# Sums of input-matrix products formed on TensorE by accumulated matmuls with the identity and its negative

## The chip, the core and the metric

The kernel runs on one NeuronCore of a Trainium2 chip. Five engines work from queues of their own and meet only at semaphores: TensorE (PE in the profile, with its weight loads as PEld), VectorE (DVE), ScalarE (ACT), GpSimd (POOL) and SyncE (SP), which here only issues DMAs. Each engine takes its instructions strictly in the order in which the program lists them. An instruction whose input isn't ready holds up all that stand behind it on the same engine. The metric is the device time of one execution in microseconds (us).

## What is computed

One encoder layer on a sequence of 1024 rows of 1024 numbers, in float32. The part that matters here is the state-space mixer (S5): the first 512 channels are cut into 32 groups of 16, each with 64 complex states in two directions.

```python
def s5_direction(uf, lam_re, lam_im, log_dt, b_re, b_im, c_re, c_im, reverse):
    ...
    lam_bar = jnp.exp(lam * dt)
    b = lax.complex(b_re.astype(f32), b_im.astype(f32))
    b_bar = ((lam_bar - 1.0) / lam)[..., None] * b
    c = lax.complex(c_re.astype(f32), c_im.astype(f32))
    bu = jnp.einsum('gph,blgh->blgp', b_bar, uf)
    a = jnp.broadcast_to(lam_bar, (1, uf.shape[1]) + lam_bar.shape)
    _, states = lax.associative_scan(_ssm_combine, (a, bu), reverse=reverse, axis=1)
    return jnp.einsum('ghp,blgp->blgh', c, states).real
...
def reference(x, ...):
    xn = rmsnorm(h, g_mix[i])
    proj = xn @ w_in[i]
    u = proj[..., :D_SSM]
    v = proj[..., D_SSM:]
    y_ssm = s5_mixer(u, ...)
    y_fft = fourier_mixer(v, w_fourier[i])
    h = h + jnp.concatenate([y_ssm, y_fft], axis=-1) @ w_out[i]
    h = h + conv_ffn(rmsnorm(h, g_ffn[i]), ...)
return rmsnorm(h, g_final)
```

The product of a complex factor with a complex input matrix has a real part that is a difference of two products and an imaginary part that is a sum of two products. These 2 x 16 differences and sums are what the change is about.

## The kernel before

The program is written as a list of steps, the string `SEQ`, whose tokens name a function and its arguments: `P:5` is `prep(5)`, `I:5` is `inputs(5)`, `S:5` is `states(5)`, `O:5` is `outputs(5)`, `U` and `VI` are products with the input projection, `WB` products with the output projection, `FA`, `FB`, `FC` the Fourier part. The order in which the steps are written gives each instruction its priority. A scheduler of the language then lays the instructions of each engine in a row by a timeline of its own, so the final order on each engine is fixed when the program is built and isn't read from the source. A second table, `OPT`, says of some 400 small operations whether they run on VectorE (`V`) or GpSimd (`G`).

The time falls into three stages. Up to about 81 us the input is normalised and transposed, the projection starts, and tables of the state-space poles are worked out. From 81 to about 335 us the state-space gather runs: 16 batches of two groups each, among products of the projections (tiles `pin` and `pwo` in PSUM) and the Fourier part. From there to the end follow the gate of the mixer (`pg`), the upward product of the feed-forward part (`u`), and the downward one (`dqa`, `dqb`).

In the gather a batch b goes through these steps. Buffer numbers are left out by the profile, so all batches show under one name.

- `prep(b)`, lines 658 to 683, is where the change lies. For the real part (i = 0) and the imaginary part (i = 1) a vector multiplication writes the products of the factor table `gst` and the raw matrix `rawb` into a tile `b` of 128x512 (line 666). It holds two halves of 256 columns. A second vector operation takes the difference or the sum of the halves into the tile `bt` (line 667); `bt` has one buffer. TensorE transposes the four 128x128 blocks of `bt` into the PSUM tile `pbm` (line 672), ScalarE copies it to `bm`. TensorE also multiplies each block of `bt` with `cbr` or `cbi`, the output matrices of the group, into `pk` (line 677, recorded as the helper's line 130), and ScalarE copies the result to `kf` and `kb`.
- `inputs(b)`: TensorE multiplies `bm` with the inputs `u` into `ps` (line 733).
- `states(b)`: VectorE multiplies `ps` with a phase table into `r` (line 745), adds halves into `scd`, runs four scans into `so` (lines 756 and 757), multiplies into `x` (line 763) and adds into `yy` (line 764). Some of these run on GpSimd.
- `outputs(b)`: TensorE forms `py` from `tm`, `u`, `yy` and the table `cm` (which `out_matrix` makes with `c` and `cm`, lines 721 to 725).

The tiles `b`, `r` and `x` take their buffers from one pool with the tag `t2`; a new tile waits until a buffer's last reader is done. Before, the tag has two buffers. All of `pbm`, `pk`, `ps` and `py` take turns in four PSUM banks. TensorE's order holds the `pin` and `pwo` matmuls, which depend on nothing in the gather, between the gather's own matmuls.

Of the kernel before, what the change touches and what calls it, by code (L numbers as in the profile page):

```python
# [11 lines left out]
F32 = mybir.dt.float32  # L12
# [3 lines left out]
AF = mybir.ActivationFunctionType  # L16
ALU = mybir.AluOpType
# [3 lines left out]
P = 128  # L21
# [9 lines left out]
LA = 4  # L31
NBM = 3
NTM = 2
NWP = 5
NSPLIT = 9
NTAB = 1026
# [45 lines left out]
def bc(ap, axis, n):  # L82
    ap = ap.unsqueeze(axis)
    shape = list(ap.shape)
    shape[axis] = n
    return ap.broadcast_to(shape)
# [3 lines left out]
def encoder_block(  # L90
# [8 lines left out]
    V, A, PE, GP = nc.vector, nc.scalar, nc.tensor, nc.gpsimd  # L99
# [3 lines left out]
    const = ctx.enter_context(tc.tile_pool(name="const", bufs=1))  # L103
# [5 lines left out]
    def opt(key, default):  # L109
        v = OPT.get(key, default)  # L110
        return {"V": V, "G": GP}.get(v, v) if isinstance(v, str) else v
# [7 lines left out]
    def bank2(name):  # L119
        return ps.tile([P, 512], F32, name=name, tag="bank_b")  # L120

    def after(ins, prev):
        tc.add_manual_dep(
            ins.ins, prev.ins.name,
            mybir.DependencyInfo(mybir.DependencyClass.NoSync, mybir.DependencyReason.DATA),
            reason="issue order",
        )

    def mm(o, lhsT, rhs, start, stop, key=None, skip=False):
        i = PE.matmul(o, lhsT, rhs, start=start, stop=stop, skip_group_check=skip)  # L130
        last_mm[0] = i
        if key is not None:
            if key in chain:
                after(i, chain[key])
            chain[key] = i
        return i
# [3 lines left out]

    ident = const.tile([P, P], F32, name="ident")
    make_identity(nc, ident)

    def gbc_dma(src, t):
        return nc.sync.dma_start(t, src.partition_broadcast(P))
# [7 lines left out]
    def split(dst_hi, dst_lo, src, eng=V):  # L153
        A.activation(dst_hi, src, AF.Copy)  # L154
        return eng.tensor_sub(dst_lo, src, dst_hi.bitcast(F32))  # L155
# [8 lines left out]
    def load_split(src, a, name, w=None, eng=V, g=None, geng=None):  # L164
# [10 lines left out]
        if w is None:  # L175
            w = outer.tile([P, 2, 512], F32R, name=name, tag="wp", bufs=NWP)
        split(w[:, 0], w[:, 1], st, eng)
# [71 lines left out]
    def q(name, shape=(P, G), dt=F32, tag="q", bufs=13):  # L249
        return sp.tile(list(shape), dt, name=name, tag=tag, bufs=bufs)  # L250

    def keep(name, shape=(P, G), dt=F32):
        return sp.tile(list(shape), dt, name=name)

    NG = 2
    NB = G // NG
# [83 lines left out]
    def pair(a):  # L340
        return a.rearrange("p (b g) -> p b g", g=NG)
# [4 lines left out]
    gst = keep("gst", (P, 8, NB, 3, NG))  # L346
# [35 lines left out]
    def cmul(eng, outr, outi, ar, ai, br_, bi_, ta, tb):  # L382

        eng.tensor_mul(ta, ar, br_)
        eng.tensor_mul(tb, ai, bi_)
        eng.tensor_sub(outr, ta, tb)
        eng.tensor_mul(ta, ar, bi_)
        eng.tensor_mul(tb, ai, br_)
        eng.tensor_add(outi, ta, tb)

    def csq(c, s_, name):

        a, b, c2, s2 = (q(f"{name}_{k}") for k in "abcs")
        V.tensor_sub(a, c, s_)
        V.tensor_add(b, c, s_)
        V.scalar_tensor_tensor(s2, c, 2.0, s_, ALU.mult, ALU.mult)
        V.tensor_mul(c2, a, b)
        return c2, s2
# [96 lines left out]
    def phase_tables(lv):  # L495
        wt_ = w1t if lv == 4 else w2t
        te = opt(f"ph{lv}", GP)
        if lv == 4:
            ec, es, ecn = (prv[k] for k in ("ec", "es", "ecn"))
            esd = q("esd")  # L500
            V.tensor_copy(esd[0:64], es[0:64])
            V.tensor_copy(esd[64:128], ecn[64:128])
            prv["cur"] = (ec, esd)
        cur = prv["cur"]
        wr, wi = wt_[:, :, 0], wt_[:, :, 1]
        if lv == 2:
            GP.memset(wr[:, :, :, 0], 1.0)
            GP.memset(wi[:, :, :, 0], 0.0)
        for j in range(lv):
            n = 1 << j  # L510
            tw = q(f"tw{lv}_{j}", (P, 2, NB, NG, 8), tag="t3" if te is GP else "t2", bufs=1 if te is GP else 2)
            cmul(te, wr[:, :, :, n:2 * n], wi[:, :, :, n:2 * n], wr[:, :, :, :n], wi[:, :, :, :n],
                 bc(pair(cur[0]), 3, n), bc(pair(cur[1]), 3, n), tw[:, 0, :, :, :n], tw[:, 1, :, :, :n])
            cur = csq(cur[0], cur[1], f"wq{lv}_{j}")
        prv["cur"] = cur
        if lv == 2:
            GP.tensor_copy(w2t[:, :, 2], w2t[:, :, 0])

    def in_factors():
        fr, fi = prv["fr"], prv["fi"]  # L520
        gt = q("gt", (P, 4, 8, G), tag="tm", bufs=NTM)
        gr_, gi_ = gt[:, 0], gt[:, 1]
# [6 lines left out]
    def out_factors():  # L529
        ec, ecn = prv["ec"], prv["ecn"]  # L530
        pt_ = q("pt", (P, 4, 8, G), tag="tm", bufs=NTM)
        cmul(V, pt_[:, 0], pt_[:, 1], pwr, pwi, bc(ec, 1, 8), bc(ecn, 1, 8), pt_[:, 2], pt_[:, 3])
# [6 lines left out]
    scd = keep("scd", (P, 2, NG, W))  # L539
    scr = keep("scr", (P, NG, W))  # L540
    cbr = keep("cbr", (P, 8, 2, 16))
    cbi = keep("cbi", (P, 8, 2, 16))

    def zeros():
        nc.sync.dma_start(dmk[96:128], dmask)
        for t in (scd, scr, cbr, cbi):
            GP.memset(t, 0.0)

    cw = const.tile([P, 188], F32, name="cw")
    rawb = keep("rawb", (P, NB, 2, NG, 16))  # L550
    rawc = keep("rawc", (P, NB, 2, NG, 16))
# [83 lines left out]
        cts[ct].u = u  # L635

    def t2(name):
        return q(name, (P, 2 * NG * P), tag="t2", bufs=2)

    def prep_ct(ct):  # L640

        for dst, i in ((cbr, 0), (cbi, 1)):
            for d in range(2):
                hs = slice(64 * d, 64 * d + 64)
                A.activation(
                    dst[hs, :, d].rearrange("p (b g) h -> p b g h", g=NG),
                    rawc[hs, 4 * ct:4 * ct + 4, i], AF.Copy)
        cts[ct].kf = q(f"kf{ct}", (P, 8, 16), tag="kf", bufs=1)
        cts[ct].kb = q(f"kb{ct}", (P, 8, 16), tag="kb", bufs=1)

    def slots(a, b, swap=0):

        return bc(a[:, :, b, swap:swap + 2].rearrange("p s i g -> p (i g) s"), 3, 16)

    def heads(a, b):
        return bc(a[:, b].rearrange("p i g h -> p (i g) h"), 2, 8)

    def prep(b):

        c, ct, sb = bs[b], b // 4, b % 4  # L660
        if sb == 0:
            prep_ct(ct)
        bt = q(f"bt{b}", (P, 2, NG, 8, 16), tag="bt", bufs=1)
        for i, op in ((0, ALU.subtract), (1, ALU.add)):
            m = t2(f"b{b}_{i}").rearrange("p (n s h) -> p n s h", n=2 * NG, s=8)
            opt(f"pb{b}{i}", V).tensor_mul(m, slots(gst, b, i), heads(rawb, b))
            opt(f"pa{b}{i}", V).tensor_tensor(bt[:, i], m[:, 0:NG], m[:, NG:2 * NG], op)
        c.bm = q(f"bm{b}", (P, 2, NG, P), tag="bm", bufs=NBM)
        pt = bank2(f"pbm{b}")
        btv = bt.rearrange("p i g s h -> p (i g) (s h)")  # L670
        for n in range(2 * NG):
            PE.transpose(pt[:, n * P:(n + 1) * P], btv[:, n], ident)
        A.activation(c.bm.rearrange("p i g n -> p (i g n)"), pt, AF.Copy)
        pk = bank2(f"pk{b}")
        for g in range(NG):
            for i, cc in ((0, cbr), (1, cbi)):
                mm(pk[:, g * 32:(g + 1) * 32], btv[:, i * NG + g],
                   cc[:, NG * sb + g].rearrange("p d h -> p (d h)"), start=(i == 0), stop=(i == 1), key=f"pk{b}")
        pkv = pk[:, :NG * 32].rearrange("p (g d h) -> p g d h", g=NG, d=2)
        A.activation(cts[ct].kf[:, NG * sb:NG * sb + NG], pkv[:, :, 0], AF.Copy)  # L680
        A.activation(cts[ct].kb[:, NG * sb:NG * sb + NG], pkv[:, :, 1], AF.Copy)
        if sb == 3:
            toeplitz(ct)

    def toeplitz(ct):
# [12 lines left out]
        nc.sync.dma_start(kd[0:P], kf.rearrange("p g h -> p (g h)"))  # L698
        tm = q(f"tm{ct}", (P, 8, 8, 16), tag="tm", bufs=NTM)
        nc.sync.dma_start(tm[:, ::-1].rearrange("p t g h -> p t (g h)"),  # L700
# [277 lines left out]
    for n in range(2):  # L978
        ns_ = slice(n * 512, (n + 1) * 512)
        for m in range(4):  # L980
            pg = bank(f"pg{m}_{n}")
            first = True
            for k in range(4):
                for wi, zi in ((0, 0), (0, 1), (1, 0)):
                    mm(pg, wg[k][:, wi, m * P:(m + 1) * P], zf[:, k, zi, ns_],
                       start=first, stop=(k == 3 and wi == 1))
# [90 lines left out]
    def operand(t, name, w=None, e=V):  # L1077
        if w is None:
            w = outer.tile([P, 2, 512], F32R, name=name, tag="wp", bufs=NWP)
        split(w[:, 0], w[:, 1], t, e)  # L1080
# [107 lines left out]
    pb = ctx.enter_context(tc.tile_pool(name="pb", bufs=1, reuse_waits="tile"))  # L1188
# [191 lines left out]
    for i in range(2):  # L1380
        w = outer.tile([P, 2, 512], F32R, name=f"du{i}", tag="wp", bufs=NWP).bitcast(F32)
        u2.extend((w[:, 0], w[:, 1]))
# [68 lines left out]
```

## Time and profile before

| | |
|---|---|
| median of three runs | 1064.2 us (1064.13 to 1065.19) |
| the profiled execution's own time | 1064.29 us |
| its span, from the first to the last instruction | 1062.5 us |
| TensorE busy, all 4504 matmul records | 971.6 us |
| VectorE busy, 1721 instructions | 936.6 us |
| ScalarE busy | 465.6 us |
| GpSimd busy | 232.8 us |

A profile shows one execution. An engine's busy time counts the instructions on it; matmuls overlap each other in TensorE, so the distance from one matmul's start to the next one's is its price, rather than its recorded duration. One float32 matmul of this kernel leaves two records, a transpose one. The granted clock is the share of its full speed that TensorE was given. "Idle before, releaser" says how long an engine stood still before an instruction and what ended that wait. A number such as `b6` in the text is the batch; it is found by counting the rows in the program's order.

### The profile page before, as it was taken

To read this page: it belongs to the slowest core of one execution; us is meant where nothing else is said; L and a number is where in the kernel's file an instruction comes from. 1 tells how busy PE (TensorE), PEld (TensorE's weight loads), DVE (VectorE), ACT (ScalarE), POOL (GpSimd) and SP (SyncE) were. 2 spreads that over 40 slices of the span, in tenths; PEclk is the share of its full clock that TensorE was granted. 3 is DMA by queue.
4 is the path that set the end of the run, shared out by engine and by line. 5 is a ranking of instruction groups with operands and counts; after the bars stand their busy time and mean duration, and the time that the engine had idled before them with its cause. 6 is when DMAs were issued, how large, how long until landed. Compare 5 with 4: busy or idle time off the path is not lost.

```text
span 1062.5 us, 13490 instructions
## 1 busy us (share of the span) xinstructions
PE 971.6 (91%) x4504; PEld 800.7 (75%) x4504; DVE 936.6 (88%) x1721; ACT 465.6 (44%) x849; POOL 232.8 (22%) x243
## 2 busy tenths in 40 slices
PE   1798978677989999999999999999999999999995
PEld 1677767666767788788888888888887778888884
DVE  6988998999997899999988889888897678999987
ACT  4444222533122656544445444454453455444644
POOL 6257556775753003200000000000000000000400
PEclk9999998878899999999999999999999989999998
DMA  7242002242021323332322322223233399847544
GB/s 242 31 146 84 26 20 91 82 150 78 24 65 51 103 96 110 94 102 77 108 86 80 100 77 71 90 80 99 73 98 117 94 363 387 308 150 244 189 129 158
DMA packets 121596, 126.78 MB, mean 119 GB/s; under 512 B 17922, under 2 KB 86455, under 8 KB 121527
## 3 DMA queue, kind: packets, MB, share of 16 engines
q1 hardware_dynamic: 121382, 125.66, 36.8%
q8 instruction: 35, 0.57, 0.2%
q14 instruction: 35, 0.28, 0.1%
q10 hardware_dynamic: 144, 0.26, 0.1%
HBM read 103.35 MB, written 22.51 MB: 118 GB/s over the span
## 4 chain that ended last, share of the span: by engine, by line
PE 46%; DVE 8%; DMA 3%; issue 1%; ACT 1%; SPq 0%; DVEq 0%; ACTq 0%
PE u L130 34%; PE dqa L130 7%; PE dqb L130 6%; DMA d_6b<-in_w_down_dram 1%; DMA d_4b<-in_w_down_dram 1%; DMA wu<-in_w_up_dram 1%; DVE hb L1325 0%; DVE cb L1235 0%; DMA d_9a<-adr 0%; DVE wo L155 0%; DVE cg L1106 0%; DMA d_8b<-in_w_down_dram 0%; DVE n_t L196 0%; DVE d_6ao L155 0%; DMA d_10b<-in_w_down_dram 0%
## 5 line engine op out<-in xcount | busy, mean ns | idle before, releaser
L1317 POOL TENSOR_TENSOR hb<-hb,gl 128x512 f32<-128x512 f32 x8 | 13.2, 1687 | 552.9 <-ACT n_sq L1290 552.9
L130 PE MATMUL u<-xb,wo 128*128 128x512 f32 x528 | 130.0, 390 | 0.2 <-ACT xb L154 0.2
L130 PEld LDWEIGHTS u<-xb,wo 128*128 128x128 f32 x528 | 99.0, 188 | 21.6 <-ACT xb L154 0.6
L130 PE MATMUL u<-xa,wo 128*128 128x512 f32 x408 | 98.8, 390 | 0.4 <-DVE wo L155 0.3
L130 PEld LDWEIGHTS u<-xa,wo 128*128 128x128 f32 x408 | 76.4, 188 | 17.1 <-DVE wo L155 0.7
L154 ACT ACTIVATE wo<-wu 128x512 fp32r<-128x512 f32 x78 | 49.1, 630 | 85.8 <-PE u L130 57.9
L130 PE MATMUL pin<-xh,win 128*128 128x512 f32 x256 | 78.2, 406 | 1.0 <-ACT xh L227 1.0
L1106 DVE SCALAR_TENSOR_TENSOR cg<-ug,cw,cg 128x896 f32<-128x896 f32 (+1 forms) x88 | 62.3, 748 | 13.2 <-ACT cg L1103 13.2
L130 PE MATMUL u<-t4o,wo 128*128 128x512 f32 x264 | 63.4, 389 | 0.0
L1106 DVE SCALAR_TENSOR_TENSOR cv<-uv,cw,cv 128x896 f32<-128x896 f32 (+1 forms) x88 | 62.1, 746 | 0.0
L154 ACT ACTIVATE wo<-ws 128x512 fp32r<-128x512 f32 x32 | 20.2, 631 | 90.2 <-PE u L130 84.6
L130 PE MATMUL pwo<-wo,yf 128*128 128x512 f32 x192 | 52.1, 421 | 7.6 <-DVE h L931 4.4
L130 PEld LDWEIGHTS u<-t4o,wo 128*128 128x128 f32 x264 | 49.6, 188 | 10.3
L130 PEld LDWEIGHTS pin<-xh,win 128*128 128x128 f32 x256 | 48.6, 194 | 10.8 <-ACT xh L227 1.4
L155 DVE TENSOR_TENSOR wo<-wu,wo 128x512 fp32r<-128x512 f32 x78 | 54.6, 700 | 0.0
L130 PE MATMUL u<-t2o,wx 128*128 128x512 f32 x204 | 49.5, 389 | 0.0
L130 PE MATMUL u<-t1o,wx 128*128 128x512 f32 x204 | 49.5, 389 | 0.0
L130 PEld LDWEIGHTS pwo<-wo,yf 128*128 128x128 f32 x192 | 36.9, 200 | 16.6 <-DVE h L931 5.0
L130 PE MATMUL pin<-xl,win 128*128 128x512 f32 x128 | 45.7, 405 | 0.1
L130 PEld LDWEIGHTS u<-t1o,wx 128*128 128x128 f32 x204 | 38.3, 188 | 7.9
L130 PEld LDWEIGHTS u<-t2o,wx 128*128 128x128 f32 x204 | 38.3, 188 | 7.9
L714 ACT ACTIVATE wt<-wt 128x128 f32<-128x128 f32 x32 | 9.9, 309 | 67.8 <-POOL wt L712 44.4
(568 smaller groups left out, 2453.7 us busy)
## 6 DMA issues: line engine op xcount, KB each, us to landing
wu<-in_w_up_dram SPq DMA_DIRECT2D x88, 256.0 KB, 3.0
adr<-cg SPq DMA_DIRECT2D x22, 512.0 KB, 3.0
xr<-in_x_dram SPq DMA_DIRECT2D x8, 512.0 KB, 8.1
win_st<-in_w_in_dram SPq DMA_DIRECT2D x16, 256.0 KB, 3.0
wo_st<-in_w_out_dram SPq DMA_DIRECT2D x16, 256.0 KB, 2.8
h<-in_x_dram SPq DMA_DIRECT2D x8, 512.0 KB, 4.3
hdr<-h SPq DMA_DIRECT2D x8, 512.0 KB, 2.6
hb<-hdr SPq DMA_DIRECT2D x8, 512.0 KB, 5.7
```

The source lines that it names most:

```text
L130: i = PE.matmul(o, lhsT, rhs, start=start, stop=stop, skip_group_check=skip)
L154: A.activation(dst_hi, src, AF.Copy)
L155: return eng.tensor_sub(dst_lo, src, dst_hi.bitcast(F32))
L714: A.activation(wf[:, :, 0:64], wf[:, :, 127:63:-1], AF.Copy, scale=(-1.0 if i else 1.0))
L1106: V.scalar_tensor_tensor(cv[:, lo:hi], src[:, at:at + hi - lo], w, cv[:, lo:hi], ALU.mult, ALU.add)
L1317: GP.tensor_mul(hv(s, n), hv(s, n), gl[:, n * 512:(n + 1) * 512])
```

## The change

`prep` no longer forms the sums. The two halves of each product tile go to TensorE as they are. Where there was one transpose of a block of `bt`, there are now two matmuls that accumulate in PSUM: the first half times the identity, and the second half times the identity, or times its negative for the real part. Where there was one matmul of a block with `cbr` or `cbi`, there are now two; for the real part the second takes `cbn`, the negative of `cbr`, which two more ScalarE copies make at each fourth batch. `bt` is gone, and the tag `t2` has four buffers in place of two.

```diff
+NT2 = 4
...
+    nident = const.tile([P, P], F32, name="nident")
+    V.tensor_scalar(nident, ident, -1.0, None, ALU.mult)
...
-            tw = q(f"tw{lv}_{j}", (P, 2, NB, NG, 8), tag="t3" if te is GP else "t2", bufs=1 if te is GP else 2)
+            tw = q(f"tw{lv}_{j}", (P, 2, NB, NG, 8), tag="t3" if te is GP else "t2", bufs=1 if te is GP else NT2)
...
+    cbn = keep("cbn", (P, 8, 2, 16))
...
-        for t in (scd, scr, cbr, cbi):
+        for t in (scd, scr, cbr, cbi, cbn):
             GP.memset(t, 0.0)
...
     def t2(name):
-        return q(name, (P, 2 * NG * P), tag="t2", bufs=2)
+        return q(name, (P, 2 * NG * P), tag="t2", bufs=NT2)
...
-        for dst, i in ((cbr, 0), (cbi, 1)):
+        for dst, i, sign in ((cbr, 0, 1.0), (cbi, 1, 1.0), (cbn, 0, -1.0)):
...
-                    rawc[hs, 4 * ct:4 * ct + 4, i], AF.Copy)
+                    rawc[hs, 4 * ct:4 * ct + 4, i], AF.Copy, scale=sign)
...
-        bt = q(f"bt{b}", (P, 2, NG, 8, 16), tag="bt", bufs=1)
-        for i, op in ((0, ALU.subtract), (1, ALU.add)):
-            m = t2(f"b{b}_{i}").rearrange("p (n s h) -> p n s h", n=2 * NG, s=8)
-            opt(f"pb{b}{i}", V).tensor_mul(m, slots(gst, b, i), heads(rawb, b))
-            opt(f"pa{b}{i}", V).tensor_tensor(bt[:, i], m[:, 0:NG], m[:, NG:2 * NG], op)
+
+        ms = []
+        for i in range(2):
+            m = t2(f"b{b}_{i}")
+            opt(f"pb{b}{i}", V).tensor_mul(m.rearrange("p (n s h) -> p n s h", n=2 * NG, s=8), slots(gst, b, i), heads(rawb, b))
+            ms.append(m.rearrange("p (j g n) -> p j g n", j=2, g=NG))
         c.bm = q(f"bm{b}", (P, 2, NG, P), tag="bm", bufs=NBM)
         pt = bank2(f"pbm{b}")
-        btv = bt.rearrange("p i g s h -> p (i g) (s h)")
-        for n in range(2 * NG):
-            PE.transpose(pt[:, n * P:(n + 1) * P], btv[:, n], ident)
+        pk = bank2(f"pk{b}")
+        for i in range(2):
+            for g in range(NG):
+                n = i * NG + g
+                for j in range(2):
+                    neg = j == 1 and i == 0
+                    mm(pt[:, n * P:(n + 1) * P], ms[i][:, j, g], nident if neg else ident, start=(j == 0), stop=(j == 1),
+                       key=f"pbm{b}")
         A.activation(c.bm.rearrange("p i g n -> p (i g n)"), pt, AF.Copy)
-        pk = bank2(f"pk{b}")
         for g in range(NG):
-            for i, cc in ((0, cbr), (1, cbi)):
-                mm(pk[:, g * 32:(g + 1) * 32], btv[:, i * NG + g],
-                   cc[:, NG * sb + g].rearrange("p d h -> p (d h)"), start=(i == 0), stop=(i == 1), key=f"pk{b}")
+            for i in range(2):
+                for j in range(2):
+                    cc = cbi if i else cbn if j else cbr
+                    mm(pk[:, g * 32:(g + 1) * 32], ms[i][:, j, g],
+                       cc[:, NG * sb + g].rearrange("p d h -> p (d h)"), start=(i == 0 and j == 0), stop=(i == 1 and j == 1),
+                       key=f"pk{b}")
```

The scheduler lays the rows anew, and that moves more than the diff names. Three places matter. The first is VectorE at the start of the gather, from the second product of batch 2 on. In these rows `b2_1` is that product, `cm1` a sum that reads GpSimd's product `c1_1`, and a number behind a name is only the buffer's. Before:

```order
L666 TENSOR_TENSOR b2_1_842<-gst_100,rawb_108 128x512
L723 TENSOR_TENSOR cm3_804<-c3_0_805 128x256
L155 TENSOR_TENSOR win4_0_1506<-win4_0_st_1504,win4_0_1506 128x512
L667 TENSOR_TENSOR bt2_838<-b2_0_839 128x256
L667 TENSOR_TENSOR bt2_838<-b2_1_842 128x256
L666 TENSOR_TENSOR b1_1_927<-gst_100,rawb_108 128x512
L725 TENSOR_TENSOR cm1_859<-c1_1_863 128x256
L721 TENSOR_TENSOR c0_0_881<-pst_101,rawc_109 128x512
```

The same place of the changed program:

```order
L671 TENSOR_TENSOR b2_1_851<-gst_102,rawb_111 128x512
L735 TENSOR_TENSOR cm3_815<-c3_0_816 128x256
L158 TENSOR_TENSOR win4_0_1549<-win4_0_st_1547,win4_0_1549 128x512
L737 TENSOR_TENSOR cm1_875<-c1_1_879 128x256
L733 TENSOR_TENSOR c0_0_897<-pst_103,rawc_112 128x512
L671 TENSOR_TENSOR b1_1_941<-gst_102,rawb_111 128x512
```

The two `bt2` rows are gone, and `b1_1` now stands behind `cm1` and `c0_0`, so nothing is left between `win4` and the row that needs GpSimd's `c1_1`.

The second place is TensorE around batch 8. `pin5` and `pin7` are products of the input projection, `ps6` is the product that VectorE reads in `states(6)`. Before:

```order
L130 MATMUL pin5_0_1744<-xl_79,win5_1_1741 128x512
L672 MATMUL pbm8_1678<-ident_70,bt8_1670 128x128 x4
L130 MATMUL pk8_1684<-cbr_105,bt8_1670 128x32
L130 MATMUL pk8_1684<-cbi_106,bt8_1670 128x32
L130 MATMUL pk8_1684<-cbr_105,bt8_1670 128x32
L130 MATMUL pk8_1684<-cbi_106,bt8_1670 128x32
L733 MATMUL ps6_1729<-u1_1217,bm6_1316 128x128 x4
L130 MATMUL pin5_1_1745<-xl_79,win5_1_1741 128x512
```

The same place of the changed program:

```order
L131 MATMUL pin7_1_1660<-xh_80,win7_1_1656 128x512
L131 MATMUL pbm8_1725<-ident_70,b8_0_1720 128x128
L131 MATMUL pbm8_1725<-nident_75,b8_0_1720 128x128
L131 MATMUL pbm8_1725<-ident_70,b8_0_1720 128x128
L131 MATMUL pbm8_1725<-nident_75,b8_0_1720 128x128
L131 MATMUL pbm8_1725<-ident_70,b8_1_1722 128x128 x4
L131 MATMUL pk8_1726<-cbr_107,b8_0_1720 128x32
L131 MATMUL pk8_1726<-cbn_108,b8_0_1720 128x32
L131 MATMUL pk8_1726<-cbi_109,b8_1_1722 128x32 x2
...
L745 MATMUL ps6_1784<-u1_1250,bm6_1351 128x128 x4
L131 MATMUL pin5_0_1799<-xh_80,win5_0_1791 128x512
```

Eight matmuls stand for four transposes and eight for four, and `ps6` now comes ahead of all of `pin5`, whose first half was done by then before. From the first matmul of `pbm6` to the last of `ps7`, TensorE's row held 85 `pin` matmuls, 16 of `pbm` and 16 of `pk`, and now holds 181, 32 and 32; `ps` (12), `py` (18) and the transposes `pyt` (8) there are as many as before. In the gather's first rows, from `pbm0` to `pbm4`, it is the other way: 74 `pin` before, 2 now.

The third place is TensorE where the gather ends. `py15` is the output of the last batch, `pwo` a product of the output projection, `pg0_0` the first product of the gate. Before:

```order
L130 MATMUL py15_2974<-tm3_2710,u3_2214 128x128
L130 MATMUL py15_2974<-cm15_2632,yy15_2870 128x128 x2
L130 MATMUL pwo_1_6_3129<-wo1_1_3_2670,yf_1925 128x512 x3
L130 MATMUL pg0_0_3175<-zf_2905,wg0_3154 128x512 x3
L130 MATMUL pg0_0_3175<-zf_2905,wg1_3159 128x512 x3
```

The same place of the changed program:

```order
L131 MATMUL py15_3066<-cm15_2719,yy15_2962 128x128 x2
L131 MATMUL pwo_1_0_3193<-wo1_1_2_2752,yf_1990 128x512
L131 MATMUL pwo_1_0_3193<-wo1_1_3_2757,yf_1990 128x512 x3
L131 MATMUL pwo_1_1_3207<-wo1_1_0_2742,yf_1990 128x512 x3
L131 MATMUL pwo_1_1_3207<-wo1_1_1_2747,yf_1990 128x512 x3
...
L131 MATMUL pwo_1_6_3221<-wo1_1_1_2747,yf_1990 128x512
L131 MATMUL pwo_1_6_3221<-wo1_1_2_2752,yf_1990 128x512 x3
L131 MATMUL pwo_1_6_3221<-wo1_1_3_2757,yf_1990 128x512 x3
L131 MATMUL pg0_0_3267<-zf_2997,wg0_3246 128x512 x3
```

Between the last `py15` and the first `pg` stood 3 `pwo` matmuls; now 28 stand there, with the eight transposes of the last output among them.

## The prediction

> **What bounds the kernel now.** I read the page first: the span, each engine's share, and the slices of the span.
>
> ```profile
> span 1062.5 us, 13490 instructions
> PE 971.6 (91%) x4504; PEld 800.7 (75%) x4504; DVE 936.6 (88%) x1721; ACT 465.6 (44%) x849; POOL 232.8 (22%) x243
> PE   1798978677989999999999999999999999999995
> DVE  6988998999997899999988889888897678999987
> PEclk9999998878899999999999999999999989999998
> ```
>
> From the 13th slice on TensorE is at 9 of 10 almost to the end. Before that, in the gather, it is at 6 to 9 while VectorE is at 9. So the table of stretches comes next (columns: busy us and count of PE, PEld, DVE, ACT and POOL, then granted clock, DMA share, GB/s). The gather is cut at two points that I need below.
>
> ```profile
> core 0: us, PE busy (x) PEld busy (x) DVE busy (x) ACT busy (x) POOL busy (x), PEclk, DMA share, GB/s
> 81.00:108.00 27.00, 23.23 (x133) 19.26 (x132) 21.99 (x27) 11.03 (x31) 20.52 (x19) 1.00 0.23 74
> 108.00:192.50 84.50, 67.14 (x357) 56.17 (x356) 78.14 (x121) 22.14 (x62) 50.33 (x59) 0.90 0.14 43
> 192.50:335.00 142.50, 118.82 (x643) 99.99 (x642) 136.65 (x224) 45.41 (x116) 94.18 (x101) 0.87 0.25 75
> ...
> 335.00:440.00 105.00, 102.67 (x484) 84.09 (x483) 91.58 (x185) 63.67 (x125) 17.23 (x12) 1.00 0.31 102
> ```
>
> From 108 to 335 us VectorE stands still for 12.2 us (6.36 and 5.85), TensorE for 41.0 (17.36 and 23.68), and TensorE's clock is 0.90 and 0.87. VectorE sets the pace of the gather. After 335 us TensorE stands still for 2.3 of 105 us, so what follows is a fixed amount of TensorE work. The end of the kernel is therefore the end of the last `py`, plus whatever TensorE still has to do then.
>
> **What goes.** The 32 sums are line 667: the group's row, and the spread of one instruction by engine.
>
> ```profile
> L667 DVE TENSOR_TENSOR bt<-b 128x256 f32<-128x256 f32 x28 | 21.8, 803 | 2.4 <-PE pk L130 2.3
> ...
> L667 DVE TENSOR_TENSOR bt<-b x28: 409/804/1490, 81.8 to 282.6; 128x256 f32<-128x256 f32 x28
> ...
> L667 POOL TENSOR_TENSOR bt<-b x4: 757/1168/1183, 124.8 to 281.9; 128x256 f32<-128x256 f32 x4
> ```
>
> VectorE loses 28 x 0.803 = 21.8 us of work. The order holds no `bt` any more, so a rival in which the change doesn't do what it says has no chance. By stretch (the same columns, of `bt` alone, ACT left out by the view):
>
> ```profile
> 81.00:108.00 27.00, 6.10 (x48) 5.51 (x48) 8.95 (x10) 0.00 (x0) 1.00 0.23 74
> 108.00:192.50 84.50, 10.82 (x74) 9.85 (x75) 5.65 (x9) 3.09 (x3) 0.90 0.14 43
> 192.50:300.00 107.50, 10.69 (x72) 9.30 (x70) 7.19 (x9) 1.18 (x1) 0.84 0.29 88
> ```
>
> That is 8.95, 5.65 and 7.19 us.
>
> **What is added.** The price of a matmul is the distance of starts in the timeline of TensorE.
>
> ```profile
> 100.02 1.07 PE L130 MATMUL pin<-xh,win 128*128 128x512 f32 x4
> 100.93 0.62 PE L130 MATMUL pin<-xl,win 128*128 128x512 f32 x2
> ...
> 104.46 0.44 PE L672 MATMUL pbm<-ident,bt 128*128 128x128 f32 x2 [0.26 <-DVE bt L667]
> 104.73 0.31 PE L130 MATMUL pk<-cbr,bt 128*128 128x32 f32 x2
> ...
> 105.10 0.39 PE L130 MATMUL pk<-cbr,bt 128*128 128x32 f32 x2
> 105.32 0.39 PE L130 MATMUL pk<-cbi,bt 128*128 128x32 f32 x2
> 105.54 1.14 PE L733 MATMUL ps<-u,bm 128*128 128x128 f32 x8
> 106.44 0.71 PE L130 MATMUL pin<-xl,win 128*128 128x512 f32 x2
> ```
>
> Four `pin` take 0.91 us, 0.2275 each. Two transposes take 0.27 us, 0.135 each. A `pk` (two records) takes 0.22 us. Four float32 matmuls of 128x128 (`ps`, eight records) take 0.90 us, 0.225 each. The new `pbm` matmuls have the shape and type of `ps`. So 64 transposes (8.6 us) become 128 matmuls (28.8 us), and 64 more `pk` cost 14.1 us: TensorE gets **34.3 us** more at full clock, 2.14 us a batch. The cover is the 41.0 us for which it stood still, if the work falls there. ScalarE, 44% busy, gets eight copies more for `cbn`; one `nident` is made before the first transpose is due. I count these at nothing.
>
> A rule speaks against this part. The Trainium skill's Perfetto Trace Analysis, section Transposes, says to use a true transpose and not a standard matmul with the identity, since the transpose skips the arithmetic. The trace agrees, 0.135 against 0.225 us. By that rule alone, with one true transpose per block kept, 20.2 of the 34.3 us would not be there, 5.0 us of them in the stretch of batches 6 to 9 below, and the sum would be lower by up to that.
>
> **First stretch, 81 to 108 us.** These are the rows of VectorE, and of GpSimd's `c`, on which the first order piece of the change turns.
>
> ```profile
> 91.88 1.31 DVE L725 TENSOR_TENSOR cm<-c 128x256 f32<-128x256 f32 x1 [1.81 <-POOL c L721]
> ...
> 97.93 1.32 DVE L710 TENSOR_TENSOR w<-w1t,w2t 128x256 f32<-128x256 f32 x1 [1.81 <-POOL cm L725]
> ...
> 101.77 0.42 DVE L710 TENSOR_TENSOR w<-w1t,w2t 128x256 f32<-128x256 f32 x1 [1.05 <-POOL wt L712]
> ...
> 107.59 1.27 DVE L745 TENSOR_TENSOR r<-ps,wt 128x512 f32<-128x512 f32 x2
> ```
>
> ```profile
> 82.72 1.28 POOL L721 TENSOR_TENSOR c<-pst,rawc 128x512 f32<-128x512 f32 x1
> 85.90 1.49 POOL L721 TENSOR_TENSOR c<-pst,rawc 128x512 f32<-128x512 f32 x1 [1.90 <-DVE cm L723]
> ...
> 90.74 1.10 POOL L721 TENSOR_TENSOR c<-pst,rawc 128x512 f32<-128x512 f32 x1
> ```
>
> Three times VectorE waits for GpSimd's chain. That chain can start only some 1.5 us earlier: its second `c` waited for VectorE's `cm` until 85.90, and could have followed its first, which ended at 84.00, after one `cm` of 0.4. So the six `bt` ahead of the wait at 101.77 turn into longer waits, and only about 1.5 us of them is gained. The two of batches 3 and 4 behind it (about 3.0 us) are gained whole. `r0`, at 107.59, comes **4.5 us earlier**, at 103.1, not 8.95. If GpSimd runs no faster, the gain is 3.0; if nothing waited, 8.95.
>
> **Second stretch, to `r7`.** By the rows' order the second product of batch 6 and `r7` are these:
>
> ```profile
> 136.75 0.68 DVE L666 TENSOR_TENSOR b<-gst,rawb 128x512 f32<-128x512 f32 x1
> ...
> 192.28 1.27 DVE L745 TENSOR_TENSOR r<-ps,wt 128x512 f32<-128x512 f32 x2
> ```
>
> From `r0` to the end of `b6` VectorE takes 137.43 - 107.59 = 29.84 us; without one `bt` (0.41) and with 0.4 of other rows moved out it is 29.0, so `b6` is ready at 132.1. From there VectorE's own way to `r7` was 54.85 us. Eight `bt` go (5.2) and 2.0 us of other rows move in: 51.6, and `r7` could start at 183.7. But the second order piece says what TensorE must do between: 181 `pin` (41.2 us), 32 `pbm` (7.2), 32 `pk` (7.0), 30 of `ps` and `py` (6.8) and eight transposes (1.0), 63.2 us, of which the first four `pbm` (0.9) can run ahead of the second product. Before, the same sum is 32.7 us against VectorE's 54.85, so TensorE was never late. Now `ps7` ends 62.3 us after `b6`, at 194.4, and VectorE waits at `r6` and `r7` for some 10.7 us. TensorE waits for `b5` and `b6` just ahead of this, and the clock of this stretch was 0.90, which cost about 0.10 x 84.5 = 8.5 us; since it now stands still only ahead of the stretch, I add a fifth of that, 1.7 us, an estimate from this row. `r7` starts at 196.1, **3.8 us later** than before. All that was gained is lost here. Bounds: 0 to 8 us later.
>
> **Third stretch, to the last `py`.** Nine `bt`, 7.19 us, go from VectorE. TensorE's row from `ps7` to the last `py` holds, by its order and the prices above, 105 us of work for some 140, so it needn't be late again. How much of 7.19 stays gained isn't shown. Nine of the shortest, 0.41 us, are 3.7 us. The rest is excess that comes beside GpSimd's work, as with the sister rows of line 666:
>
> ```profile
> L666 DVE TENSOR_TENSOR b<-gst,rawb x24: 677/1020/1725, 81.1 to 281.5; 128x512 f32<-128x512 f32 x24
> ```
>
> Either it goes with the `bt`, or it falls on other VectorE rows. Ends 3.7 and 7.2; both rows are equally near, so I take the middle, **5.4 us**. The Trainium skill's SBUF — State Buffer, section SBUF: two separate sides, says that GpSimd and a VectorE operation with two SBUF inputs take their shared port as an exclusive lock and block each other. The spread from 409 to 1490 ns agrees with it; by that rule the excess would fall on the next such row, and the gain would be nearer 3.7.
>
> **What is left over.** By the third order piece 25 more `pwo` stand between the last `py` and the gate: 25 x 0.2275 = **5.7 us** of TensorE work that was done inside the gather before. The gather's end now:
>
> ```profile
> 334.25 0.61 PE L130 MATMUL py<-cm,yy 128*128 128x128 f32 x4
> 334.62 0.94 PE L130 MATMUL pwo<-wo,yf 128*128 128x512 f32 x3
> 335.39 4.28 PE L130 MATMUL pg<-zf,wg 128*128 128x512 f32 x18
> ```
>
> TensorE ran from the last `py` into the gate without a break, so nothing there hides them.
>
> **The sum.** +3.8 - 5.4 + 5.7 = **+4.1 us**. The profiled execution took 1064.29 us, 1.8 more than its span and 0.1 from the median 1064.2. Forecast: **1068 us**, own range 1062.5 to 1073.
>
> **Rivals.** First, *the saving carries through the third stretch* (no slower, or faster). VectorE's wait at `r6` and `r7` lets GpSimd run ahead by up to 10.7 us, so that the full 7.2 us stays and half of the 5.85 us idle goes too, and `r7` comes only 1.5 later: 1.5 - 7.2 - 2.9 + 5.7 = -2.9, 1061 us. For it speaks that 94.18 us of GpSimd work lie there; against it, that 5.85 us of waits in 142.5 leave little to win. It decides where VectorE needs under 133 us from `r7` to the last `yy`.
>
> Second, *TensorE becomes the bound of the third stretch as well*. It gets about 11 us there (five batches of 2.14) beside 118.82 busy at clock 0.87, and what stood still did so waiting for the Fourier part and the batches. If none of the new work falls into the idle 23.68 us, it adds 11: 1079 us. Against it: the idle is twice the new work.
>
> A transfer that hides everything isn't in sight; DMA shares of 0.13 to 0.33 are low.
>
> **How the numbers follow.** Forecast 0.50, first rival 0.25, second 0.20, others 0.05. A measurement here can tell about 0.2%, 2.1 us, from no change: 1062.1 to 1066.3. The first rival gives 0.19 of its 0.25 to faster, the forecast 0.02, others 0.03: 0.24. Of the forecast 0.16, with 0.06 of the first rival, lies within: 0.22. Slower 0.54. The range reaches from the first rival's lower side to the second's middle, 1058 to 1080.
>
> **What would show it.** VectorE idle of about 8 us before the first `cm<-c` of line 737; `r` of batch 7 near 196 us with TensorE's `ps` as the releaser of some 11 us; a granted clock near 1 from 132 to 194; the gate's first `pg` near 339. Wrong if `r7` comes before 190 (then TensorE's row is cheaper than counted), or if TensorE is idle for under 15 us from 196 on (then the second rival).

## The result and the profile after

The change makes the kernel slower: 1082.38 us median (1079.49 to 1083.93, four runs) against 1064.7 (1064.13 to 1066.5) on the same chip, ratio 1.016 with a 95% interval of 1.0144 to 1.0175. The profiled execution took 1083.39 us. Of its page, the lines that answer to those of before:

```profile
span 1081.6 us, 14106 instructions
PE 1010.4 (93%) x4824; PEld 846.1 (78%) x4824; DVE 917.7 (85%) x1694; ACT 468.9 (43%) x857; POOL 225.2 (21%) x240
PE   2799999988979999999999999999999989999995
DVE  7995976788986779989998888889888578999987
PEclk9996989988799999999999999999999989999998
```

TensorE has 320 records more (192 of `pbm`, 128 of `pk`) and is busy 38.8 us longer, VectorE 18.9 us less. Span less busy time is how long TensorE stood still: 71.2 us in place of 90.9, 19.7 less. 38.8 - 19.7 = 19.1 us is the growth of the span. So about half of what TensorE got went into time in which it had stood still. By stretch, cut at `r0`, at `r7` and behind the last `py` (columns: busy us and count of TensorE, its weight loads, VectorE, ScalarE, GpSimd, then granted clock, DMA share, GB/s):

```profile
81.00:103.00 22.00, 19.96 (x130) 19.58 (x128) 11.00 (x15) 5.78 (x18) 15.60 (x17) 0.75 0.11 38
103.00:200.60 97.60, 95.06 (x552) 85.14 (x552) 73.26 (x114) 27.34 (x74) 48.74 (x58) 0.92 0.14 43
200.60:345.40 144.80, 126.61 (x742) 111.07 (x741) 127.28 (x209) 44.73 (x117) 92.83 (x100) 0.87 0.24 73
```

In the second stretch TensorE is busy for 95.06 of 97.60 us, and VectorE, which was the busier of the two before (78.14 of 84.50 us in the prediction's table), for 73.26. The timeline of VectorE at the points that the prediction names:

```profile
89.00 1.31 DVE L737 TENSOR_TENSOR cm<-c 128x256 f32<-128x256 f32 x1 [4.98 <-POOL c L733]
...
102.97 1.48 DVE L757 TENSOR_TENSOR r<-ps,wt 128x512 f32<-128x512 f32 x2 [2.28 <-PE pk L131]
...
167.08 1.29 DVE L757 TENSOR_TENSOR r<-ps,wt 128x512 f32<-128x512 f32 x2 [4.16 <-PE pk L131]
...
182.96 1.29 DVE L757 TENSOR_TENSOR r<-ps,wt 128x512 f32<-128x512 f32 x2 [1.56 <-PE ps L745]
...
195.21 0.42 DVE L776 TENSOR_TENSOR yy<-x 128x256 f32<-128x256 f32 x1 [6.24 <-PE py L131]
...
199.94 0.29 DVE L724 TENSOR_TENSOR wt<-w 128x128 f32<-128x128 f32 x1 [1.32 <-POOL w L722]
...
200.61 1.28 DVE L757 TENSOR_TENSOR r<-ps,wt 128x512 f32<-128x512 f32 x2
```

The first row is the sum `cm1`. Then come `r0` (102.97; before 107.59), `r5`, `r6`, a `yy`, a table `wt` and `r7` (200.61; before 192.28). From `r5` to `r7` VectorE waits for TensorE three times, for 4.16 + 1.56 + 6.24 = 11.96 us. A wait of `r` for `pk` is, by the kernel's text, one for a buffer: `r` takes the `t2` buffer of a product that `pk` must read first. TensorE's row from `pbm` of batch 6 to `ps` of batch 7, and at the end of the gather:

```profile
131.55 0.46 PE L131 MATMUL pbm<-ident,b 128*128 128x128 f32 x2 [2.54 <-DVE b L671]
...
198.50 1.14 PE L745 MATMUL ps<-u,bm 128*128 128x128 f32 x8
199.48 0.39 PE L131 MATMUL pbm<-ident,b 128*128 128x128 f32 x2
...
344.71 0.61 PE L131 MATMUL py<-cm,yy 128*128 128x128 f32 x4
345.08 5.06 PE L131 MATMUL pwo<-wo,yf 128*128 128x512 f32 x21
349.97 1.04 PE L800 MATMUL pyt<-ident,ys 128*128 128x128 f32 x8
350.77 1.85 PE L131 MATMUL pwo<-wo,yf 128*128 128x512 f32 x7
352.45 21.96 PE L131 MATMUL pg<-zf,wg 128*128 128x512 f32 x96
```

TensorE is past the last `py` at 345.08 (before 334.62), and `pg` starts at 352.45 (335.39).

### The profile page after: what moved, and what is told of

It reads as the page before. It is cut to its first block, busy times and chain, and to the rows that moved or that the text cites. A ratio compares the mean times of both kernels' runs of the same rounds, so it can differ in the third digit from the quotient of the medians.

```text
span 1081.6 us, 14106 instructions
## 1 busy us (share of the span) xinstructions
PE 1010.4 (93%) x4824; PEld 846.1 (78%) x4824; DVE 917.7 (85%) x1694; ACT 468.9 (43%) x857; POOL 225.2 (21%) x240
## 4 chain that ended last, share of the span: by engine, by line
PE 41%; DVE 10%; DMA 4%; issue 2%; ACT 1%; SPq 0%; DVEq 0%; ACTq 0%
PE u L131 34%; PE dqb L131 4%; PE dqa L131 4%; DVE cb L1247 1%; DMA wu<-in_w_up_dram 1%; DVE hb L1337 1%; DMA hb<-hdr 1%; DMA d_10b<-in_w_down_dram 1%; DMA d_7a<-adr 1%; DMA d_3a<-adr 0%; DVE d_6ao L158 0%; DVE cg L1118 0%; DVE room L1247 0%; DMA d_4b<-in_w_down_dram 0%; DVE ca L1247 0%
## 5 line engine op out<-in xcount | busy, mean ns | idle before, releaser
L157 ACT ACTIVATE wo<-ws 128x512 fp32r<-128x512 f32 x32 | 20.2, 631 | 87.8 <-PE u L131 73.8
L131 PE MATMUL pbm<-ident,b 128*128 128x128 f32 x192 | 36.1, 319 | 6.4 <-DVE b L671 4.8
```

## The experiments

Two questions are open after the comparison: is it the amount of TensorE's work or the new order of the rows (the ring of four lays them anew), and why does VectorE's saving bring so little? Each run's own ratio is against the kernel before on the same chip.

**e1, the ring alone** (with the same edit in the line of the tables `tw`, which share the tag).

```diff
-        return q(name, (P, 2 * NG * P), tag="t2", bufs=2)
+        return q(name, (P, 2 * NG * P), tag="t2", bufs=4)
```

> The kernel before, with only the ring of t2 buffers raised from 2 to 4; the sums stay on VectorE. Theory 'work' (TensorE's 34.3 us of added matmuls are the cause): nothing is added, so 1064, at most 2 us either way. Theory 'order' (the larger ring lays the rows anew, so that pin and pwo stand elsewhere): by its order 29 pwo instead of 3 stand between the last py and the gate, 26 x 0.2275 = 5.9 us, so 1070 or more.

1072.26 us, ratio 1.0066 (1.0048 to 1.0084): 7.0 us slower, with TensorE's work unchanged. "Order" holds for this part: a larger ring and the order that comes with it cost 7 us by themselves.

**e2, the change with the ring of two.**

```diff
-NT2 = 4
+NT2 = 2
```

> The change with the ring of t2 buffers kept at 2. Theory 'work': the added matmuls are all there, and a product must now wait sooner for the pk before it, so as slow as the change or slower, 1080 to 1090. Theory 'order': by its order no pwo is left over and only 57 pin stand between pbm of batch 6 and ps of batch 7 (181 in the change), so most of the 18 us comes back, 1064 to 1070.

1087.49 us, ratio 1.0205 (1.0189 to 1.0222). With no `pwo` left over and 57 `pin` in place of 181 ahead of `ps7`, the kernel is 4.8 us slower than the change, so "order" as it was put falls. The ring of four costs 7.0 us alone, and with the change it is the faster one. The ring of two may have a price of its own here, though: from 81 to 380 us VectorE waits 11.6 us for `pk` in e2 and 6.8 in the change, and e9 below, with it, is some 10 us slower than e4. So e2 alone can't say what the order is worth.

**e3, the matmuls alone** (`hident` is half the identity, and `cbr` and `cbi` are made at half their size, so the sums of two come out as before).

```diff
-            PE.transpose(pt[:, n * P:(n + 1) * P], btv[:, n], ident)
+            for j in range(2):
+                mm(pt[:, n * P:(n + 1) * P], btv[:, n], hident, start=(j == 0), stop=(j == 1), key=f"pbm{b}")
...
+                for j in range(2):
+                    mm(pk[:, g * 32:(g + 1) * 32], btv[:, i * NG + g],
+                       cc[:, NG * sb + g].rearrange("p d h -> p (d h)"), start=(i == 0 and j == 0),
+                       stop=(i == 1 and j == 1), key=f"pk{b}")
```

> The kernel before with its sums on VectorE and its ring of 2, but each pbm block by two float32 matmuls with half the identity, and each pk matmul twice with half the weights: TensorE's added 34.3 us alone, with no saving on VectorE. Theory 'work': the change's loss of 18 us is here too, and what VectorE saved in the change (about 10 us of it reached the path) is missing, so 1082 to 1095. Theory 'order': the idle 42.6 us of TensorE takes most of it; 42 pwo are left over against 3, 8.9 us, so 1070 to 1075.

1093.1 us, ratio 1.026 (1.0238 to 1.0282): 27.7 us for 34.3 us of work. "Work" holds. Its page:

```profile
span 1089.9 us, 14132 instructions
PE 1001.2 (92%) x4824; PEld 834.8 (77%) x4824; DVE 934.6 (86%) x1722; ACT 465.8 (43%) x849; POOL 227.2 (21%) x243
```

TensorE is busy 29.6 us longer, and stands still for 88.7 us, 2.2 less than before. The 44.8 us for which it stood still in the gather (81 to 335 us: 254.00 - 209.19) took almost nothing of the new work. That busy time grew by less than 34.3 has to do with the clock: less of it ran at half speed (20.5 us lost in place of 24.9, in the table below).

**e4, the sums left out and nothing put in their place.** TensorE reads the first half of each product alone, so the second summand of every input-matrix product is missing. The ring is four.

```diff
+                PE.transpose(pt[:, n * P:(n + 1) * P], ms[i][:, 0, g], ident)
...
+                mm(pk[:, g * 32:(g + 1) * 32], ms[i][:, 0, g],
+                   cc[:, NG * sb + g].rearrange("p d h -> p (d h)"), start=(i == 0), stop=(i == 1), key=f"pk{b}")
```

> The change without the second summand: pbm by one true transpose of the first half, pk by the first half alone, so TensorE's work is that of the kernel before, VectorE's sums are gone, and the ring is 4. It leaves out the second half of every input-matrix product. Theory 'work': without the added matmuls the saving shows, by the prediction's own terms 4.5 + 5.2 + 5.4, so 1049 to 1057. Theory 'order': the ring of 4 eats the saving, 1062 to 1068.

1066.36 us, ratio 1.0013 (0.9997 to 1.003). No gain against before; against e1, with the same ring, 0.0053 or 5.7 us less. e2 against e3 gives the same, 0.0055. So in these two pairs 21.8 us of VectorE's work are worth some 6 us (a third pair, e9 against before, goes the other way, see there). The gather's row in the table of stretches, first of before, then of e4:

```profile
81.00:335.00 254.00, 209.19 (x1129) 175.42 (x1128) 236.77 (x370) 78.58 (x209) 165.03 (x179) 0.89 0.21 64
```

```profile
81.00:335.00 254.00, 212.50 (x1137) 179.85 (x1137) 217.94 (x343) 76.73 (x207) 159.43 (x175) 0.88 0.21 64
```

VectorE is busy 18.8 us less in the same 254 us, and TensorE no more than 3.3 us longer. What VectorE saved became VectorE's standing still, 36 us in place of 17. The waits of VectorE in e4 name GpSimd first (what waited, for what, us in total, times, longest):

```profile
DVE cm L730 <- POOL c L728: 7.4, 2, 4.5
DVE cm L732 <- POOL c L728: 5.2, 2, 3.9
```

**e5 and e6, GpSimd relieved (both on e4).** e5 (the same for the products `w` and `tw`, which share the tag):

```diff
-            m = q(f"c{b}_{i}", (P, 2 * NG, 8, 16), tag="t3", bufs=1)
+            m = q(f"c{b}_{i}", (P, 2 * NG, 8, 16), tag="t3", bufs=2)
```

> As the run with the sums left out (which leaves out the second half of every input-matrix product), with two t3 buffers instead of one, so that a product of the tables or output matrices needn't wait for the sum of the one before it on the other engine. Theory 'GpSimd': VectorE's saved 21.8 us were waited away for GpSimd (22.1 us of waits from 81 us on, 9.4 before), so these waits fall below 12 us and the time falls by 8 or more, to 1052 to 1059. Theory 'TensorE's other waits': TensorE's idle comes from the Fourier part and from the order of fillers, so nothing changes, 1064 to 1069.

e6:

```diff
+OPT.update({f"{p}{b}{i}": "V" for p in ("td", "ta") for b in range(16) for i in range(2)})
```

> As the run with the sums left out (the second half of every input-matrix product is missing), with all sums of cm and wt on VectorE: 17 and 24 of them leave GpSimd, some 27 us of its work, and VectorE gets 17 x 0.42 + 24 x 0.29 = 14 us. Theory 'GpSimd': GpSimd was the engine waited for, so its relief is worth more than VectorE's 14 us, which fit into its idle 35 us: 1056 to 1062. Theory 'TensorE's other waits': 1064 to 1072.

1063.87 us, ratio 0.9993 (0.9982 to 1.0004), and 1063.63, ratio 0.999 (0.9978 to 1.0002). "GpSimd" falls by the forecast times. In e5 the waits went as expected, and the time didn't follow: from 81 to 380 us VectorE waits 9.1 us for GpSimd in place of 22.1, no such wait is over 2.4 us any more, and another is at the head.

```profile
DVE h L938 <- PE pwo L131: 8.8, 4, 2.7
DVE c L728 <- POOL wt L719: 2.4, 1, 2.4
```

In e6 most of these waits stay, 17.6 us, so it tests less than e5. And e5's edit alone costs the kernel before 6 us (e8), which may hide a gain of that size. TensorE's longest waits from 81 to 380 us, first in e4, then in e5:

```profile
PE pbm L679 <- DVE b L671: 17.7, 7, 6.0
PE pwo L131 <- DVE wo L158: 3.8, 1, 3.8
```

```profile
PE pbm L679 <- DVE b L671: 9.0, 10, 3.5
PE pwo L131 <- ACT yf L157: 7.4, 1, 7.4
```

The wait of `pbm` for the product `b` is half as long in e5, a wait for `yf` comes up in its place, and TensorE's standing still as a whole stays (89.4 and 90.3 us).

**e7 and e8, two `t3` buffers in the change and in the kernel before** (the edit of e5).

> The change with two t3 buffers. Theory 'GpSimd': of VectorE's waits for GpSimd (23.7 us) half goes, but its waits for TensorE (20.3 us) stay, so 1072 to 1079. Theory 'TensorE's other waits': 1080 to 1085.

> The kernel before with two t3 buffers and nothing else, as a control. Both theories: VectorE waited 9.4 us for GpSimd and was busy 93% from 81 to 335 us, so little is to be had, 1061 to 1066.

e7: 1083.83 us, ratio 1.0182 (1.0152 to 1.0213), no gain. e8: 1071.07 us, ratio 1.0055 (1.0036 to 1.0074); neither theory expected a loss. Like e1 it gives the kernel before more buffers and a new order, and costs 6 us.

**e9, e4 with the ring of two** (`NT2 = 2`).

> The sums left out (the second half of every input-matrix product is missing) with the ring of t2 buffers at 2, as in the kernel before, so without the 7 us that the larger ring cost alone. Theory 'VectorE's saving is worth about 6 us' (the ring of 4 cost 7.0 alone and 1.3 with the sums left out): 1056 to 1060. Theory 'TensorE's standing still doesn't depend on the sums': 1062 to 1067. Theory 'two buffers are too few once the products stay in them until TensorE has read them': 1068 or more.

1075.74 us, ratio 1.0106 (1.0083 to 1.0128): by its time the third case. Without `bt` the products hold their buffers until TensorE has read them. The trace shows 4.5 us in which VectorE waits for `pk` (from 81 to 345 us; none in e4) and a longer wait of `pbm` for `b` (22.0 us; 17.7 in e4); that the two buffers make up all of the 10 us between e9 and e4 isn't shown. Against the kernel before, which also has two, leaving the sums out costs 11 us here.

**e10, the change with `pin` moved behind `ps7`** (`VI:0` also stands three tokens sooner).

```diff
...
-I:5 T:6 VI:2 OM:6 S:4 T:7 O:2 O:3 VI:0 P:7 VI:3 P:8 FA:0 S:5 I:6 VI:1 O:4 P:9 S:6 LU:2 I:7 OM:7
+I:5 T:6 OM:6 S:4 VI:0 T:7 O:2 O:3 P:7 P:8 FA:0 S:5 I:6 O:4 P:9 S:6 LU:2 I:7 VI:1 VI:3 VI:2 OM:7
...
```

> The change with three of the four projections of the Fourier part (VI:2, VI:3, VI:1) named behind the inputs of batch 7 in the priority order: by the order 96 instead of 181 pin stand between pbm of batch 6 and ps of batch 7, so 85 x 0.2275 = 19.3 us of TensorE's row move behind ps of batch 7, where TensorE stood still for some 20 us. Theory 'order': r7 comes 12 to 19 us sooner and the pin fill those waits, 1064 to 1074. Theory 'work' (TensorE's row is full, and what it stands still for are the Fourier part and the batches): r7 comes sooner, but the time does not, 1078 to 1088.

1079.11 us, ratio 1.0137 (1.0117 to 1.0156). "Work" holds: the time is in its range, with no clear gain on the change (1.016, 1.0144 to 1.0175). VectorE reaches `r7` 13 us sooner than in the change:

```profile
187.66 1.28 DVE L749 TENSOR_TENSOR r<-ps,wt 128x512 f32<-128x512 f32 x2
```

and TensorE comes to the last `py` here:

```profile
332.55 0.61 PE L123 MATMUL py<-cm,yy 128*128 128x128 f32 x4
332.92 5.04 PE L123 MATMUL pwo<-wo,yf 128*128 128x512 f32 x21
337.80 1.04 PE L792 MATMUL pyt<-ident,ys 128*128 128x128 f32 x8
338.59 9.10 PE L123 MATMUL pwo<-wo,yf 128*128 128x512 f32 x39
347.53 1.75 PE L123 MATMUL pg<-zf,wg 128*128 128x512 f32 x7
```

The gather ends at 332.92, sooner than in the kernel before (334.62), and the kernel is still 15 us slower than that one: 60 `pwo` wait behind it in place of 3.

**e11, `pk` alone** (the second half of e3's edit).

> The kernel before, with its sums and true transposes, and each pk matmul twice with half the weights: 64 x 0.22 = 14.1 of the 34.3 us alone. Theory 'work': the loss goes with the work, 14.1/34.3 of the 27.7 us of both, 11 us, so 1073 to 1078. Theory 'order or chain' (the loss is that of pbm, which stands on the way to ps, while nobody waits long for pk): 1064 to 1069.

1076.8 us, ratio 1.0106 (1.0083 to 1.0129): 11.3 us for 14.1 us of work, as "work" had it. The rest of e3, 27.7 - 11.3 = 16.4 us, belongs to the 20.2 us of `pbm`. Either kind costs about 0.8 us per us, e11's interval alone allowing 0.6 to 1.0.

**e12, e4 with the products named sooner** (each of `P:5` to `P:15` four tokens, `NT2 = 6`).

> The sums left out (the second half of every input-matrix product is missing), with P:5 to P:15 each named four tokens sooner in the priority order and a ring of 6 t2 buffers to hold the products. With the sums left out, TensorE's largest wait was 17.7 us of pbm for the product b, though VectorE stood still for 36 us. Theory 'late products': b stands too late in VectorE's row, so with it sooner TensorE's waits for b fall below 9 us and the time falls with them, 1052 to 1059. Theory 'another wait takes its place': the waits for b fall, but TensorE's standing still as a whole stays within 4 us of before, and the time is 1061 to 1068.

1068.37 us, ratio 1.0038 (1.0022 to 1.0055). Inconclusive: TensorE's waits of `pbm` for `b` stayed at 16.6 us, so the edit didn't do what it was to test. The rows of e5 above answer in part: there that wait did halve, and another took its place.

All runs by TensorE's parts. Busy and span are from each page, still is span less busy. The traces show a granted clock of either 1.00 or 0.50, in turns, and "lost" is the part of busy that half clock cost: in each half microsecond of the trace, busy time times (1 - granted clock), summed. "Work" is busy less lost, the time at full clock. These columns are of the profiled execution, which can lie some us from the median (e8 1067.62 against 1071.07, e11 1079.67 against 1076.8); the ratios are of all runs.

| kernel | ratio | busy | lost | work | still | span |
|---|---|---|---|---|---|---|
| before | 1 | 971.6 | 24.9 | 946.7 | 90.9 | 1062.5 |
| the change | 1.016 | 1010.4 | 33.2 | 977.2 | 71.2 | 1081.6 |
| e1 ring of 4 alone | 1.0066 | 968.9 | 24.7 | 944.2 | 101.7 | 1070.6 |
| e2 change, ring of 2 | 1.0205 | 1002.4 | 21.5 | 980.9 | 82.8 | 1085.2 |
| e3 matmuls alone | 1.026 | 1001.2 | 20.5 | 980.7 | 88.7 | 1089.9 |
| e4 sums left out | 1.0013 | 973.1 | 29.0 | 944.1 | 89.4 | 1062.5 |
| e5 e4, two t3 | 0.9993 | 971.7 | 24.7 | 947.0 | 90.3 | 1062.0 |
| e6 e4, sums of cm, wt on VectorE | 0.999 | 971.8 | 26.2 | 945.6 | 91.8 | 1063.6 |
| e7 change, two t3 | 1.0182 | 1002.3 | 24.1 | 978.2 | 80.1 | 1082.4 |
| e8 before, two t3 | 1.0055 | 967.2 | 21.3 | 945.9 | 98.6 | 1065.8 |
| e9 e4, ring of 2 | 1.0106 | 973.3 | 27.0 | 946.3 | 98.7 | 1072.0 |
| e10 change, pin later | 1.0137 | 1003.7 | 25.4 | 978.3 | 73.7 | 1077.4 |
| e11 pk alone | 1.0106 | 987.2 | 26.9 | 960.3 | 90.7 | 1077.9 |
| e12 e4, products sooner | 1.0038 | 975.9 | 30.0 | 945.9 | 91.3 | 1067.2 |

Every kernel with the new matmuls has 977 to 981 us of work, every one without any of them 944 to 947: 30 to 37 us for the 34.3 that were counted, whatever the order. Only the four with the new matmuls and without the sums (the change, e2, e7, e10) stand still for less than 88 us. What the change added is 30.5 us of work and 8.3 us lost to half clock, less 19.7 us of standing still.

## Why the prediction was wrong

The direction was right, the size was not: 1082 in place of 1068, 9.4 us above the forecast's own range and 2.4 above the wide one. The nearest number was the second rival's (1079), with a chance of 0.20. By the steps, as far as spans of the two profiled executions show them: `r0` 4.6 us earlier, from `r0` to `r7` 12.9 longer, to the last `py` 2.1 longer, from there to the first `u` (407.14 before, 424.39 after) 6.8 longer, and 1.9 to the end, together 19.1.

- **The prices were right.** Starts of `pbm` stand 0.22 us apart at full clock, as `ps` did. One product slipped: 28 x 0.803 is 22.5, and the 21.8 that the sum goes on with is the row's own busy time. The row of 63.2 us was right too: from 131.55 to 199.48 TensorE was busy throughout, 67.9 us, and 5.1 of these went to the clock (below), which leaves 62.8.

```profile
131.55:199.48 67.93, 67.93 (x378) 60.21 (x378) 46.14 (x73) 18.73 (x47) 33.83 (x42) 0.92 0.15 44
```

- **First stretch: the sum right, its parts not.** `r0` came 4.6 us earlier (forecast 4.5). But the wait at `cm` was 4.98 us, not 8 (GpSimd's second `c` started at 83.50 in place of 85.90), and 2.28 us went to a wait for `pk` that the forecast didn't have. That the two balanced was luck.
- **Second stretch: mechanism right, one term too small.** `r7` came at 200.61, not 196.1. VectorE waited for TensorE for 12 us, as forecast, though at `r5`, `r6` and a `yy` rather than at `r6` and `r7`, so the listed sign named the wrong rows. The term that was too small is the clock, "I add a fifth of that, 1.7 us"; the sign "a granted clock near 1 from 132 to 194" didn't come. The row of TensorE's half clock in this stretch, and one from the stretch ahead of it:

```profile
132.82:143.06 10.24, 10.24 (x41) 9.37 (x41) 9.54 (x16) 2.32 (x8) 4.96 (x8) 0.50 0.01 2
91.90:108.90 17.00, 17.00 (x79) 16.81 (x79) 10.69 (x16) 5.05 (x17) 9.20 (x12) 0.50 0.03 6
```

  10.24 us busy at half clock lose 5.1 us, 3.4 more than counted, and `ps7` was done at 199.48, 3.4 later than the 196.1. The last 1.1 us goes with the wait of `wt` for GpSimd's `w` that ended at 199.94. The longer window ahead of `b6` lost TensorE 8.5 us more; what that did to the time isn't shown.
- **Third stretch: this step failed, by 7.5 us, the largest miss.** The forecast had a gain of 5.4 from VectorE's 7.19 us of `bt`, since TensorE's row "holds 105 us of work for some 140, so it needn't be late again". The stretch took 144.47 us from `r7` to the last `py`, 2.1 longer than before. What failed is that VectorE sets the pace there, so that what it saves carries to the end. VectorE did have 9.6 us less to do (127.28 in place of 136.84, in the window 200.60 to 345.40 and in 192.30 to 335.00 of before), but it stood still for 17.5 us in place of 5.9. TensorE was busy for 126.61 us and stood still for 18.19, and by the measure of the table it lost 16.8 us to half clock. 126.6 - 16.8 = 109.8 us of work, so the 105 was 4.8 short; and the 35 us taken for room were lost clock and standing still, which had been there before (16.3 and 23.7 us, beside 102.7 of work) and mostly stayed. Of the 7.1 us more of work 5.5 did fall into time in which TensorE had stood still, and what VectorE saved was waited away. Why it waits there isn't settled by a run. Its longest waits in this stretch, of which the one for `pe` was 1.8 us before:

```profile
DVE yfs L900 <- PE pe L131: 5.2, 1, 5.2
DVE cm L737 <- POOL c L733: 1.8, 1, 1.8
```

  The second rival isn't what happened either, though its number is near: it had none of the new work fall into the idle time. And neither sign of being wrong came: `r7` was at 200.61, not before 190, and TensorE's 18.19 us of idle are more than 15.
- **What is left over: right, then 3.0 us more.** 25 more `pwo` stand behind the last `py`, as forecast (5.7 of the 6.8 us to the first `u`). Behind the gate 1.5 us of waits for `wo` came up that weren't there before, and 1.9 us more fell between the first `u` and the end. So the miss is 4.5 + 7.5 + 3.0 = 15.0 us, 19.1 against 4.1.
- **The view behind all of it** was "VectorE sets the pace of the gather". e4 speaks against it: with VectorE's 21.8 us gone and TensorE's work as before, the kernel is no faster than before, and only 5.7 us faster than with the ring alone. Behind 335 us TensorE stands still for only 18 of 727.5 us before, so a shorter gather mainly leaves more `pwo` behind it, as e10 shows. The time is TensorE's work, its lost clock and its standing still. The first rival, that the saving carries, falls with the third stretch.
- **The Trainium skill's rule** against matmuls with the identity (Perfetto Trace Analysis, Transposes) points the right way: the `pbm` part, 64 true transposes made into 128 matmuls, costs about 16 of the 27.7 us in e3.

Two things stay open. What TensorE's remaining 90 us of standing still hang on when the sums are gone isn't settled: with VectorE's waits for GpSimd cut from 22.1 to 9.1 us, and the wait of `pbm` halved, it was the same (e5), and e12 didn't reach that wait. And the parts don't add: the new matmuls cost 27.7 us in e3, 10.5 between e9 and e2, and some 16 between e4 and the change; matmuls, ring and saving measured one by one make 27.7 + 7.0 - 6 = 29 us, and the change costs 17. Each edit lays the rows anew, and an edit of the buffers alone moves the time by 6 or 7 us (e1, e8); new order and new buffers weren't tried apart. No version here beats the kernel before by more than the noise, not even those that form no sums at all (e4, e5, e6), so in the orders that were tried nothing was to be had by forming the sums elsewhere.

## What to carry to other kernels

Where one engine is saturated for the rest of the program, work added to it ahead of that point can be paid nearly in full, though it stood still for 45 us beside it: 27.7 us for 34.3 in e3, where the standing still took 2.2 us and the rest of the difference came from the clock. Where the other engine's work went at the same time it cost less, 0.3 to 0.5 us per us. Work taken off another engine is worth only what it takes off the first one's standing still (6 of 21.8 us, with buffers enough), though that other engine was 93% busy. Before counting the gap between an engine's work and its stretch as cover, take its lost clock and its known waits out of the gap. And where a scheduler lays the rows, run the side edit (here the buffers) alone: it may cost several us by itself.

## What the hardware showed unexpectedly

The granted clock stayed at half for 17 us (91.9 to 108.9, the row above) while TensorE's row ran without a gap, mostly with short float32 matmuls. In e10, whose row reads the same there, it did so for 17.07 us again, in e7 for 6.8. The longest such window in the gather of the kernel before was 10.24 us, and TensorE was busy for 8.66 of it. The Trainium skill's page TensorE: Matmul & The Clock Gate, section "What's actually happening", has full speed return after one busy window of about 3.4 us. The windows here are indeed multiples of some 3.41 us (10.24 / 3, 17.07 / 5), but five of them in a row were busy, so the measurement differs. The short matmuls alone aren't the cause: in e7 the same kind of run, `pbm` and `pk` of the next batches, went at full clock.

```profile
98.50:109.00 10.50, 10.50 (x94) 10.42 (x94) 6.95 (x10) 4.40 (x15) 3.12 (x5) 1.00 0.03 9
```

What held the clock down in the change and in e10 isn't known.
